# Moving the first loads, the root tables, the last rows and one store of a hybrid decoder step

## The chip, the cores and the metric

The kernel runs on one core of a Trainium2 chip. The core has a matrix engine (TensorE, PE in the rows; its weight loads are PEld), a vector engine (VectorE, DVE), a scalar engine for functions and copies (ScalarE, ACT), a slower general engine (GpSimd, POOL), and a queue engine (SyncE, SP) that issues most transfers. A "q" behind an engine's name is its sequencer: waiting, and issuing transfers. The metric is device microseconds (us) for one execution; lower is better.

## The reference

One decoder layer for 1024 prompt tokens and 8 sampled tokens, width 1024. All of it but two places lies outside the change: the norm at the very start and the norm at the very end.

```python
def _rms_norm(x, g):
    xf = x.astype(jnp.float32)
    y = xf * lax.rsqrt(jnp.mean(xf * xf, axis=-1, keepdims=True) + EPS)
    return (y * g.astype(jnp.float32)).astype(x.dtype)
...
    h = _rms_norm(x, norm_mix)
    proj = jnp.einsum('bld,de->ble', h, w_in).astype(f32)
...
    pe = jnp.einsum('blp,pd->bld', p, w_pl_proj)
    x = x + pe * jax.nn.sigmoid(jnp.einsum('bld,de->ble', _rms_norm(x, norm_pl), w_pl_gate))
...
        return _rms_norm(x, norm_final), [jnp.stack(lst) for lst in new]
```

## The kernel before

Tokens are cut into nine tiles: eight of 128 prompt tokens and one of the 8 sampled ones. Inside, activations lie with the 1024 features on the partitions (eight blocks of 128) and the 1032 tokens along the row, split into a high and a low part, so that each dense product is three matmuls (`mm`, line 69): weight-high by act-high, weight-high by act-low, weight-low by act-high. A weight slice of 1024 x 128 is loaded as `wraw`, cast to `wh` on ScalarE (line 138), and the rest `wl` is formed on VectorE (line 139). `dense` runs over token chunks of 344.

**Opening.** SP asks for the token tiles `xt` (line 210), and between them for the norm gains (`gain_cols`, five small loads into `r0`, line 117) and three narrow column slices of `w_in` (line 216, into `wsm`, 48 columns in use). Then come three groups of three token tiles (`PARTS`). Per tile: the sum of squares on ScalarE (line 224), the root (line 225), the reciprocal and the scaled copy `xn` on VectorE (lines 226, 227). Per group and feature block k: three transposes of `xn` on TensorE into a PSUM tile (line 233), then the high part on ScalarE (line 235) and the low part on VectorE (line 236), both with the gain column of the block. The first products, for `wsm`, and those of the first gate slices run between the groups as soon as their chunk is there.

**Ending.** The last token group (264 tokens) goes through eight gate products. For each, `gate_add` scales on VectorE (line 1276), takes the sigmoid on ScalarE (line 1277), multiplies by `pe` (line 1280) and adds to the residual `x2` (line 1281; its tile is called `acc` in the rows). Then `final(tt)` for the tiles 6, 7 and 8 (tile 8 has the 8 sampled rows): transposes back (line 1294), two halves of a sum of squares (line 1296), the root (line 1298), the reciprocal (line 1299), the scaling with the final gain `gf` (line 1302) and a store (line 1303).

The framework's scheduler sets the order of instructions on each engine from the order of the code and from dependencies; each engine runs its own list strictly in that order, and waits on counters of the other engines. Of two activations that need different function tables (square, copy and root live in one, sigmoid in another) a table load stands ahead of the second.

Of the kernel before, what the change touches and what calls it, by code (L numbers as in the profile page):

```python
# [8 lines left out]
F32 = mybir.dt.float32  # L9
F32R = mybir.dt.float32r  # L10
AF = mybir.ActivationFunctionType
ALU = mybir.AluOpType
# [4 lines left out]
P = 128  # L17
# [6 lines left out]
PARTS = ((0, 384), (384, 384), (768, 264))  # L24
# [15 lines left out]
def hybrid_step(  # L40
# [9 lines left out]
    V, S, G, TE = nc.vector, nc.scalar, nc.gpsimd, nc.tensor  # L50
    dma = nc.sync.dma_start
# [4 lines left out]
    cp = ctx.enter_context(tc.tile_pool(name="cp", bufs=1, reuse_waits="tile"))  # L56
# [12 lines left out]
        TE.matmul(o, l, r, start=start, stop=stop)  # L69


    ident = cp.tile([P, P], F32, name="ident")
    make_identity(nc, ident)
    ones = cp.tile([P, P], F32, name="ones")
# [31 lines left out]
    def gain(base, k):  # L106
        return gcols[:, base + k : base + k + 1]
# [6 lines left out]
    def gain_cols(pool):  # L114
        r0 = pool.tile([41, P], F32, name="r0")
        for src, o, n in ((norm_mix, 0, 8), (norm_ffn, 8, 8), (norm_pl, 16, 8), (ssm_norm, 24, 16), (gdn_norm, 40, 1)):
            dma(r0[o : o + n, :], src[0].rearrange("(k p) -> k p", p=P))
        to_cols(r0, gcols, 41)

    def conv_cols(pool):  # L120
        r1 = pool.tile([120, P], F32, name="r1")
        for j in range(4):
            dma(r1[24 * j : 24 * j + 24, :], ssm_conv_w[0][j].rearrange("(k p) -> k p", p=P))
        dma(r1[96:120, :], ssm_conv_b[0].rearrange("(k p) -> k p", p=P))
        r2 = pool.tile([96, P], F32, name="r2")
        for j in range(4):
            dma(r2[24 * j : 24 * j + 24, :], gdn_conv_w[0][j].rearrange("(k p) -> k p", p=P))
        to_cols(r1, cwm, 120)
        to_cols(r2, cwg, 96)
# [72 lines left out]
    with (  # L202
        tc.tile_pool(name="p0", bufs=1, side="right", reuse_waits="tile") as p0,
        tc.tile_pool(name="p0x", bufs=4, side="right", reuse_waits="tile") as p0x,
    ):
        xts = []
        for tt in range(9):
            n = P if tt < 8 else NB
            xt = p0x.tile([P, D], F32, name="xt", bufs=9)
            dma(xt[:n], x_prompt[0, tt * P : tt * P + P, :] if tt < 8 else x_sample[:, 0, :])  # L210
            xts.append(xt)
            if tt == 0:
                gain_cols(p0)
            if tt == 3:
                for o, c0, m in ((0, COL_DT, 32), (R_B, COL_BETA, 8), (R_A, COL_A, 8)):
                    dma(wsm[:, :, o : o + m], w_in[:, c0 : c0 + m].rearrange("(k p) f -> p k f", p=P))
        for g in range(3):
            t0, tn = PARTS[g]
            xns = []
            for tt in range(3 * g, 3 * g + 3):  # L220
                n, xt = (P if tt < 8 else NB), xts[tt]
                xn = p0x.tile([P, D], F32, name="xn", bufs=6)
                ss = p0x.tile([P, 1], F32, name="ss", bufs=9)
                S.activation(xn[:n], xt[:n], AF.Square, accum_out=ss[:n])
                S.activation(ss[:n], ss[:n], AF.Sqrt, bias=b_eps[:n], scale=1.0 / D)
                V.reciprocal(ss[:n], ss[:n])
                V.tensor_scalar(xn[:n], xt[:n], ss[:n], None, ALU.mult)
                xns.append((xn, n))
            for k in range(KD):
                pool, name = ((pt, "pt"), (py, "py"), (pz, "pz"), (pt, "pt"), (py, "py"))[k % 5]  # L230
                t = pool.tile([P, 512], F32, name=name)
                for j, (xn, n) in enumerate(xns):
                    TE.transpose(t[:, j * P : j * P + n], xn[:n, k * P : k * P + P], ident[:n, :n])
                h, l = (a[:, t0 : t0 + tn] for a in hacts[k])
                S.activation(h, t[:, :tn], AF.Copy, scale=gain(G_MIX, k))
                V.scalar_tensor_tensor(l, t[:, :tn], gain(G_MIX, k), h.bitcast(F32), ALU.mult, ALU.subtract)
        conv_cols(p0)
# [72 lines left out]
    with tc.tile_pool(name="pr", bufs=1, side="right", reuse_waits="tile") as pr:  # L310
# [67 lines left out]
        for hh in range(2):  # L378
            q = slice(64 * hh, 64 * hh + 64)
# [711 lines left out]
    for tt in range(9):  # L1091
        n = P if tt < 8 else NB
# [3 lines left out]
        for k in range(2):  # L1096
            TE.transpose(t[:, k * P : k * P + n], pr_[:n, k * P : k * P + P], ident[:n, :n])
            ts = slice(tt * P, tt * P + n)
# [44 lines left out]
    for f in range(8):  # L1143
# [16 lines left out]
        if 1 <= f < 5:  # L1160
            q = 2 * (f - 1)
# [21 lines left out]
    def roots(sqs, rb, t0, tn):  # L1183

        ts = slice(t0, t0 + tn)
        t = pt.tile([P, 512], F32, name="pt")
        G.tensor_tensor(rb[:, ts], rb[:, ts], sqs[:, ts], ALU.add)
        mm(t[:, :tn], ones, rb[:, ts])
        S.activation(rb[:, ts], t[:, :tn], AF.Sqrt, bias=b_eps, scale=1.0 / D)
        V.reciprocal(rb[:, ts], rb[:, ts])  # L1190
# [73 lines left out]
    gf = nrm.tile([P, D], F32, name="gf")  # L1264
    dma(gf, norm_final.partition_broadcast(P))

    def gate_add(f, t0, tn, o):

        ts = slice(t0, t0 + tn)
        if t0 < PARTS[2][0] and f < 2:  # L1270
            if f == 0:
                roots(sqs2, rb2, t0, tn)
            elif t0 == 0:
                roots(sqs2, rb2, *PARTS[2])
        gt = b2.tile([P, 384], F32, name="pg", tag="sg")
        V.tensor_tensor(gt[:, :tn], rb2[:, ts], o, ALU.mult)  # L1276
        S.activation(gt[:, :tn], gt[:, :tn], AF.Sigmoid)
        pe_ = b2.tile([P, 384], F32, name="pe2", tag="xf")
        dma(pe_[:, :tn], pe_d[f, :, ts])
        V.tensor_tensor(gt[:, :tn], gt[:, :tn], pe_[:, :tn], ALU.mult)  # L1280
        V.tensor_tensor(x2[:, f, ts], x2[:, f, ts], gt[:, :tn], ALU.add)

    def final(tt):
        n = P if tt < 8 else NB
        ts = slice(tt * P, tt * P + n)
        ss = nrm.tile([P, 3], F32, name="fss", bufs=3)
        xo = b2.tile([P, D], F32, name="xo", tag="xf" if tt == 8 else "lt")
        halves = []
        for q in range(2):
            pool, name = (pd, "pd") if tt == 8 else ((pt, "pt"), (py, "py"))[q]  # L1290
            t = pool.tile([P, 512], F32, name=name)
            halves.append(t)
            for k in range(4):
                TE.transpose(t[:n, k * P : k * P + P], x2[:, 4 * q + k, ts], ident)
            sq = b2.tile([P, 512], F32, name="fsq", tag="sg")
            S.activation(sq[:n], t[:n], AF.Square, accum_out=ss[:n, q : q + 1])
        V.tensor_tensor(ss[:n, 2:3], ss[:n, 0:1], ss[:n, 1:2], ALU.add)
        S.activation(ss[:n, 2:3], ss[:n, 2:3], AF.Sqrt, bias=b_eps[:n], scale=1.0 / D)
        V.reciprocal(ss[:n, 2:3], ss[:n, 2:3])
        for q in range(2):  # L1300
            c = slice(512 * q, 512 * q + 512)
            V.scalar_tensor_tensor(xo[:n, c], halves[q][:n], ss[:n, 2:3], gf[:n, c], ALU.mult, ALU.mult)  # L1302
        dma(y_prompt[0, ts, :] if tt < 8 else y_sample[:, 0, :], xo[:n])


    for part in (PARTS[:2], PARTS[2:]):
        for f in range(8):
            if len(gws) == f:
                w = slb.tile([P, 2, 8, P], F32R, name="gw", tag="parts")
                with tc.high_priority(offset=2000):  # L1310
                    raw = wp.tile([P, 8, P], F32, name="wraw")
                    dma(raw, w_pl_gate[:, f * P : f * P + P].rearrange("(k p) f -> p k f", p=P))
                    S.copy(w[:, 0], raw)  # L1313
                    V.tensor_tensor(w[:, 1], raw, w[:, 0].bitcast(F32), ALU.subtract)  # L1314
                gws.append([(w[:, 0, k], w[:, 1, k]) for k in range(8)])
            dense(gws[f], h3acts, lambda t0, tn, o: gate_add(f, t0, tn, o), part)
        for tt in range(6) if len(part) == 2 else range(6, 9):
            final(tt)
# [38 lines left out]
```

## Time and profile before

| | |
|---|---|
| median of three runs | 2700.68 us (2695.79 to 2703.67) |
| the profiled execution: its time / its span | 2698.8 us / 2697.1 us |
| TensorE busy | 2628.7 us, 97% of the span |
| VectorE, ScalarE, GpSimd busy | 57%, 38%, 10% |
| first transpose of a token tile | 10.74 us |
| first dense product | 18.01 us |
| last dense product ends | about 2683.3 us |

Times within the trace count from the span's start. Between the first dense product and the last TensorE has hardly a gap, so the change is read in two places: the 18 us ahead of the first product with the 20 us behind it, and the 14 us behind the last product.

### The profile page before, as it was taken

How to read it: one execution, taken by the hardware profiler on the slowest of the kernel's cores; microseconds unless marked ns; L12 is line 12 of the kernel's file. 1: busy time of each engine (PE TensorE's matmuls, PEld its weight loads, DVE VectorE, ACT ScalarE, POOL GpSimd, SP SyncE). 2: the span in 40 equal slices, each digit the busy share in tenths (PEclk: the TensorE clock that was granted, in tenths of full speed). 3: DMA queues.
4: the chain of work that ended last, by engine and by line, in shares of the span. 5: the costliest groups of instructions: out<-in, count | busy, mean ns of one | idle time of the engine just before them, and what ended most of it. 6: DMA issues, size and time to landing. Idle time of an engine off the chain costs nothing.

```text
span 2697.1 us, 43777 instructions
## 1 busy us (share of the span) xinstructions
PE 2628.7 (97%) x17431; PEld 2544.5 (94%) x17431; DVE 1546.1 (57%) x2757; ACT 1024.8 (38%) x2080; POOL 256.9 (10%) x495
## 2 busy tenths in 40 slices
PE   7999999999989999999999999999999999999998
PEld 7999999989989899898999999999999999999998
DVE  6677897588657576565445575434343333333465
ACT  5555556364364373343332235322112121212243
POOL 0111222121110110210000000010000000000020
PEclk9999999999999999999999999999999999999999
DMA  3345445455453453477664457411111111111122
GB/s 123 119 151 173 140 154 157 105 116 153 112 127 114 104 149 101 103 209 200 189 187 139 117 183 246 128 45 46 42 53 44 51 44 51 44 52 43 45 89 94
DMA packets 456666, 306.34 MB, mean 114 GB/s; under 512 B 44049, under 2 KB 430010, under 8 KB 455438
## 3 DMA queue, kind: packets, MB, share of 16 engines
q1 hardware_dynamic: 454062, 295.13, 38.5%
q10 hardware_dynamic: 2400, 8.42, 0.8%
q8 instruction: 137, 2.24, 0.3%
q14 instruction: 67, 0.55, 0.1%
HBM read 227.17 MB, written 76.31 MB: 113 GB/s over the span
## 4 chain that ended last, share of the span: by engine, by line
PE 49%; DVE 1%; DMA 1%; ACT 1%; issue 1%; SPq 0%; DVEq 0%; ACTq 0%
PE pd L69 45%; PE py L69 2%; PE pt L69 1%; DMA wraw<-in_w_pl_gate_dram 0%; PE pt L1139 0%; DMA kg<-ktok_d 0%; PE pz L69 0%; DVE gw L1314 0%; PE pt L968 0%; DMA pr<-in_p_prompt_dram 0%; DMA wraw<-in_w_pl_proj_dram 0%; DVE y L187 0%; DMA mg<-y_d 0%; DVE xo L1302 0%; ACT gw L1313 0%
## 5 line engine op out<-in xcount | busy, mean ns | idle before, releaser
L69 PE MATMUL pd<-h,wh 128*128 128x344 f32 x6384 | 1542.4, 323 | 18.3 <-ACT wh L138 11.1
L69 PEld LDWEIGHTS pd<-h,wh 128*128 128x128 f32 x6384 | 1106.4, 189 | 31.7 <-ACT wh L138 13.4
L69 PE MATMUL pd<-h,wl 128*128 128x344 f32 x3192 | 1030.7, 323 | 1.8 <-DVE wl L139 0.7
L69 PEld LDWEIGHTS pd<-h,wl 128*128 128x128 f32 x3192 | 602.8, 189 | 7.0 <-DVE wl L139 5.3
L138 ACT CAST wh<-wraw 128x512 fp32r<-128x512 f32 (+1 forms) x386 | 234.4, 609 | 847.5 <-PE pd L69 812.4
L139 DVE TENSOR_TENSOR wl<-wraw,wh 128x512 fp32r<-128x512 f32 (+1 forms) x386 | 265.1, 688 | 342.2 <-ACT wh L138 338.5
L69 PE MATMUL pd<-gu,wh 128*128 128x344 f32 (+2 forms) x1056 | 249.2, 320 | 0.1
L69 PE MATMUL pd<-y,wh 128*128 128x344 f32 x768 | 187.7, 325 | 0.0
L69 PEld LDWEIGHTS pd<-gu,wh 128*128 128x128 f32 x1056 | 182.3, 188 | 0.5 <-DVE acc L1195 0.4
L69 PE MATMUL pd<-gu,wl 128*128 128x344 f32 (+2 forms) x528 | 168.9, 320 | 0.0
L709 ACT ACTIVATE ab<-ab,ncolA 128x128 f32<-128x128 f32 x256 | 81.8, 391 | 142.1 <-POOL ab L705 136.0
L69 PEld LDWEIGHTS pd<-y,wh 128*128 128x128 f32 x768 | 133.4, 190 | 1.2 <-issue 0.2
L69 PE MATMUL pd<-y,wl 128*128 128x344 f32 x384 | 125.2, 326 | 0.0
L1246 DVE TENSOR_TENSOR acc<-acc,pd 128x344 f32<-128x344 f32 x120 | 61.2, 512 | 103.9 <-PE pd L69 103.5
L422 ACT COPY raw<-pd 128x344 f32<-128x344 f32 x144 | 62.5, 438 | 149.6 <-PE pd L69 137.2
L1181 POOL TENSOR_TENSOR sqs<-sqs,sqt 128x1032 f32<-128x1032 f32 x12 | 30.5, 2542 | 923.9 <-ACT sqt L1180 923.9
L1225 DVE TENSOR_TENSOR lt<-rb,pd 128x344 f32<-128x344 f32 x66 | 33.8, 513 | 141.2 <-PE pd L69 141.2
L69 PEld LDWEIGHTS pd<-gu,wl 128*128 128x128 f32 x528 | 99.2, 188 | 0.0
L436 DVE SCALAR_TENSOR_TENSOR ca<-raw,cwm,ca 128x1056 f32<-128x1056 f32 x72 | 95.9, 1332 | 2.0
L436 DVE SCALAR_TENSOR_TENSOR ca<-raw,cwg,ca 128x1056 f32<-128x1056 f32 x72 | 96.5, 1341 | 0.8
L69 PE MATMUL pd<-h,gw 128*128 128x384 f32 (+1 forms) x576 | 94.3, 322 | 1.5 <-DVE pg L1276 1.5
L69 PEld LDWEIGHTS pd<-h,gw 128*128 128x128 f32 x576 | 91.2, 188 | 2.5 <-DVE pg L1276 1.9
(391 smaller groups left out, 3458.1 us busy)
## 6 DMA issues: line engine op xcount, KB each, us to landing
wraw<-in_w_in_dram SPq DMA_DIRECT2D x88, 512.0 KB
wraw<-in_w_ffn_in_dram SPq DMA_DIRECT2D x44, 512.0 KB
ab<-acum_d SPq DMA_DIRECT2D x32, 512.0 KB
out_dram<-sd SPq DMA_DIRECT2D x48, 256.0 KB
wraw<-in_w_ffn_out_dram SPq DMA_DIRECT2D x40, 256.0 KB
sg_d<-mg SPq DMA_DIRECT2D x16, 516.0 KB
bb<-rk_d SPq DMA_DIRECT2D x8, 1024.0 KB
sd<-in_state_ssm_dram SPq DMA_DIRECT2D x32, 256.0 KB
```

What stands on the lines that cost most here:

```text
L69: TE.matmul(o, l, r, start=start, stop=stop)
L138: S.copy(wh[:, :n], raw[:, k0 : k0 + n])
L139: V.tensor_tensor(wl[:, :n], raw[:, k0 : k0 + n], wh[:, :n].bitcast(F32), ALU.subtract)
L422: S.copy(raw[:, 3 + t0 : 3 + t0 + n], o[:, :n])
L436: V.scalar_tensor_tensor(ca, raw[:, j : j + CONVN], w[j], ca, ALU.mult, ALU.add)
L709: S.activation(ab[:, h], ab[:, h], AF.Exp, bias=ncolA[:, c, h0 + h : h0 + h + 1])
L1181: G.tensor_tensor(sqs[:, ts], sqs[:, ts], sq[:, :tn], ALU.add)
L1225: V.tensor_tensor(dst[:, t0 : t0 + tn], rb[:, t0 : t0 + tn], o, ALU.mult)
L1246: V.tensor_tensor(a, a, o, ALU.add)
```

## The change

Four edits. (1) The first three token tiles are asked for ahead of the gain vectors, and the narrow slices of `w_in` move one tile further back. (2) A tiny tile `warm` is set, and a square root of it stands first on ScalarE, so that the table with the root is the one loaded first. (3) Behind the last sigmoid of the kernel another tiny root, of the first column of `gt`, brings the same table back. (4) In `final`, the rows of tile 8 are scaled by the reciprocal on ScalarE and multiplied by the final gain on GpSimd, and the store of tile 7 is issued from ScalarE's queue.

```diff
+    warm = cp.tile([P, 2], F32, name="warm")
+    V.memset(warm, 1.0)
+    S.activation(warm[:, 0:1], warm[:, 0:1], AF.Sqrt)
     ident = cp.tile([P, P], F32, name="ident")
...
-            if tt == 0:
+            if tt == 2:
                 gain_cols(p0)
-            if tt == 3:
+            if tt == 4:
                 for o, c0, m in ((0, COL_DT, 32), (R_B, COL_BETA, 8), (R_A, COL_A, 8)):
                     dma(wsm[:, :, o : o + m], w_in[:, c0 : c0 + m].rearrange("(k p) f -> p k f", p=P))
...
         S.activation(gt[:, :tn], gt[:, :tn], AF.Sigmoid)
+        if f == 7 and t0 == PARTS[2][0]:
+            S.activation(warm[:, 1:2], gt[:, 0:1], AF.Sqrt)
...
-            V.scalar_tensor_tensor(xo[:n, c], halves[q][:n], ss[:n, 2:3], gf[:n, c], ALU.mult, ALU.mult)
-        dma(y_prompt[0, ts, :] if tt < 8 else y_sample[:, 0, :], xo[:n])
+            if tt == 8:
+                S.activation(xo[:n, c], halves[q][:n], AF.Copy, scale=ss[:n, 2:3])
+                G.tensor_tensor(xo[:n, c], xo[:n, c], gf[:n, c], ALU.mult)
+            else:
+                V.scalar_tensor_tensor(xo[:n, c], halves[q][:n], ss[:n, 2:3], gf[:n, c], ALU.mult, ALU.mult)
+        (S.dma_start if tt == 7 else dma)(y_prompt[0, ts, :] if tt < 8 else y_sample[:, 0, :], xo[:n])
```

Line numbers behind the first edit are higher by three in the changed kernel, and by more behind the others. The head of SP's list, with the counters that each transfer waits for (transfers report to eight completion counters in turn, DMAHW0 to DMAHW7, so that the ninth waits for the first), before:

```order
L210 DMA xt<-in_x_prompt_dram 128x1024
L117 DMA r_113<-in_norm_mix_dram 8x128
L117 DMA r_113<-in_norm_ffn_dram 8x128
...
L146 DMA wraw<-in_w_in_dram 128x8x128 [waits DMAHW1_49]
L216 DMA wraw<-in_w_in_dram 128x8x32 [waits DMAHW2_49,Pool_49]
```

and in the changed kernel:

```order
L213 DMA xt<-in_x_prompt_dram 128x1024 x3
L120 DMA r_120<-in_norm_mix_dram 8x128
...
L213 DMA xt<-in_x_prompt_dram 128x1024 [waits DMAHW0_49]
L149 DMA wraw<-in_w_in_dram 128x8x128 [waits DMAHW1_49]
L213 DMA xt<-in_x_prompt_dram 128x1024 [waits DMAHW2_49]
L219 DMA wraw<-in_w_in_dram 128x8x32 [waits DMAHW3_49,Pool_49]
```

Three tiles now stand at the head; the fifth tile waits for the third to have landed, and the narrow slices stand behind it.

The head of ScalarE's list, without waits (`xn,ss` is the sum of squares of a token tile, `ss` alone the root, `h` the high part), before:

```order
L224 ACT_TABLE_LOAD
L224 ACTIVATE xn,ss<-xt 128x1024 x2
L225 ACT_TABLE_LOAD
L225 ACTIVATE ss<-ss,b_eps 128x1 x2
L224 ACTIVATE xn,ss<-xt 128x1024
L225 ACTIVATE ss<-ss,b_eps 128x1
L224 ACTIVATE xn,ss<-xt 128x1024
L235 ACTIVATE h_101<-pt,gcols 128x384
...
L225 ACTIVATE ss<-ss,b_eps 128x1
L138 CAST wh<-wraw 128x512
L224 ACTIVATE xn,ss<-xt 128x1024
```

and in the changed kernel:

```order
L74 ACT_TABLE_LOAD
L74 ACTIVATE warm<-warm 128x1
L227 ACTIVATE xn,ss<-xt 128x1024 x3
L228 ACTIVATE ss<-ss,b_eps 128x1 x3
L227 ACTIVATE xn,ss<-xt 128x1024
L238 ACTIVATE h_104<-pt,gcols 128x384
...
L228 ACTIVATE ss<-ss,b_eps 128x1
L227 ACTIVATE xn,ss<-xt 128x1024
L141 CAST wh<-wraw 128x512
```

One table load is gone; the first three roots stand behind the third square; and the square of the fifth tile has moved ahead of the first cast of a weight.

The end of the lists of ScalarE and then of VectorE and GpSimd in the changed kernel, with waits (`Activation` counts ScalarE's finished instructions; before, ScalarE's list has the table load behind the two squares, VectorE's ends with two scalings of `xo<-pd` 8x512, and GpSimd's has nothing here):

```order
L1280 ACTIVATE pg<-pg 128x264 [waits DVE_49]
L1282 ACT_TABLE_LOAD
L1282 ACTIVATE warm<-pg 128x1 [waits Activation_49]
L1301 ACTIVATE fsq,fss<-py 128x512 [waits PE_49]
...
L1303 ACTIVATE fss<-fss,b_eps 8x1 [waits DVE_49]
L1312 DMA out_dram<-xo 128x1024 [waits DMAHW4_49,DVE_49]
L1308 ACTIVATE xo<-pd,fss 8x512 [waits DMAHW5_49,DMAHW3_49,DMAHW7_49,DMAHW1_49,DVE_49]
L1308 ACTIVATE xo<-pd,fss 8x512
```

```order
L1285 TENSOR_TENSOR pg<-pg,pe_26022 128x264 [waits DMAHW2_49,Activation_49]
L1286 TENSOR_TENSOR acc<-acc,pg 128x264 [waits DVE_49]
...
L1304 RECIPROCAL fss<-fss 8x1 [waits Activation_49]
```

The tiny root reads `pg`, which the multiply on VectorE then overwrites, so that the multiply's count on ScalarE is one higher than before: it waits for the tiny root too. The two copies of tile 8 stand behind the store of tile 7 on ScalarE, and the last work ahead of the last store is now GpSimd's.

## Rows read from the trace of the kernel before

**Rows 1.** The page, its first part: busy time, share, instructions.

```profile
PE 2628.7 (97%) x17431; PEld 2544.5 (94%) x17431; DVE 1546.1 (57%) x2757; ACT 1024.8 (38%) x2080; POOL 256.9 (10%) x495
```

**Rows 2.** Windows: length, PE, PEld, DVE, ACT, POOL busy, PEclk, DMA share, GB/s.

```profile
2.00:4.00 2.00, 0.00 (x0) 0.00 (x0) 0.98 (x3) 0.09 (x1) 0.64 (x3) 1.00 0.74 263
4.00:11.00 7.00, 0.56 (x2) 0.44 (x3) 1.40 (x5) 5.14 (x10) 0.00 (x0) 1.00 0.97 312
6.00:7.00 1.00, 0.00 (x0) 0.00 (x0) 0.00 (x0) 0.06 (x1) 0.00 (x0) 1.00 1.04 406
18.00:24.20 6.20, 6.13 (x21) 5.61 (x22) 5.29 (x12) 5.70 (x13) 0.13 (x2) 0.51 0.49 141
24.20:40.00 15.80, 15.56 (x102) 13.40 (x100) 10.83 (x27) 9.42 (x22) 0.15 (x2) 1.00 0.04 9
```

**Rows 3.** Timeline of SP's queue, opening: start, length, what, count.

```profile
0.82 0.39 SPq L210 DMA_DIRECT2D xt<-in_x_prompt_dram  x1
3.00 1.70 SPq L210 DMA_DIRECT2D xt<-in_x_prompt_dram  x3
5.29 6.37 SPq L216 DMA_DIRECT2D wraw<-in_w_in_dram  x3
```

**Rows 4.** Timeline of ScalarE, opening; in brackets idle time before and releaser.

```profile
4.38 1.06 ACT L224 ACTIVATE xn<-xt 128x1024 f32<-128x1024 f32 x1 [2.28 <-DMA xt<-in_x_prompt_dram]
...
6.94 1.06 ACT L224 ACTIVATE xn<-xt 128x1024 f32<-128x1024 f32 x1 [1.42 <-DMA xt<-in_x_prompt_dram]
...
8.11 1.28 ACT L225 ACT_TABLE_LOAD   x1
...
13.39 0.58 ACT L235 ACTIVATE h<-pt,gcols 128x384 fp32r<-128x384 f32 x1 [1.10 <-PE pt L233]
...
17.29 0.67 ACT L138 CAST wh<-wraw 128x512 fp32r<-128x512 f32 x1
...
25.70 0.58 ACT L235 ACTIVATE h<-pt,gcols 128x384 fp32r<-128x384 f32 x1 [2.00 <-PE pt L233]
```

**Rows 5.** Timeline of VectorE, the last two token tiles of the opening.

```profile
31.18 1.40 DVE L227 TENSOR_SCALAR xn<-xt,ss 128x1024 f32<-128x1024 f32 x2
```

**Rows 6.** Timeline of TensorE, opening.

```profile
10.74 0.47 PE L233 MATMUL pt<-ident,xn 128*128 128x128 f32 x1 [5.01 <-DVE xn L227]
...
12.93 0.42 PE L233 MATMUL pt<-ident,xn 128*128 128x128 f32 x1
...
18.01 0.94 PE L69 MATMUL pd<-h,wh 128*128 128x344 f32 x2 [1.74 <-ACT wh L138]
```

**Rows 7.** Timeline of ScalarE, ending.

```profile
2684.37 0.41 ACT L1277 ACTIVATE pg<-pg 128x264 f32<-128x264 f32 x1
...
2687.48 1.28 ACT L1298 ACT_TABLE_LOAD   x1
2688.77 0.29 ACT L1298 ACTIVATE fss<-fss,b_eps 128x1 f32<-128x1 f32 x1
```

**Rows 8.** Timeline of VectorE, ending.

```profile
2684.81 0.43 DVE L1280 TENSOR_TENSOR pg<-pg,pe 128x264 f32<-128x264 f32 x1 [1.04 <-ACT pg L1277]
...
2692.06 0.74 DVE L1302 SCALAR_TENSOR_TENSOR xo<-py,fss,gf 128x512 f32<-128x512 f32 x1
...
2692.89 1.40 DVE L1302 SCALAR_TENSOR_TENSOR xo<-pd,fss,gf 8x512 f32<-8x512 f32 x2
```

**Rows 9.** Timeline of SP's queue, ending: the last three stores, first start, whole length.

```profile
2690.79 3.82 SPq L1303 DMA_DIRECT2D out_dram<-xo  x3
```

**Rows 10.** Groups by shape, GpSimd: count, busy us, mean ns, idle before and releaser.

```profile
L1187 POOL TENSOR_TENSOR rb<-rb,sqs 128x384 f32<-128x384 f32 x2 | 3.2, 1604 | 0.1
L1187 POOL TENSOR_TENSOR rb<-rb,sqs 128x344 f32<-128x344 f32 x3 | 2.9, 980 | 5.6 <-ACT rb L1177 5.5
...
L1187 POOL TENSOR_TENSOR rb<-rb,sqs 128x264 f32<-128x264 f32 x1 | 0.8, 761 | 2.9 <-ACT rb L1177 2.9
```

## The prediction

> **What bounds the kernel now.** The page's busy shares come first: TensorE is busy 2628.7 us of a span of 2697.1 us [rows 1]. So a change that leaves the middle as it is can only move the two ends, and I read these engine by engine on the timeline.
>
> In the opening the reader is to see a chain. The first token tile is squared at 4.38 us, the second, which was asked for only at 3.00 us behind the gains, at 6.94 us [rows 3, 4]. Behind it a table load of 1.28 us holds the first root until 9.39 us [rows 4]. The first scaled tile reaches TensorE at 10.74 us, and the first PSUM tile is complete after twelve transposes, the last of them at 12.93 us [rows 6]; ScalarE takes it over at 13.39 us, makes eight high parts, and casts the first weight at 17.29 us [rows 4]. TensorE's first product starts at 18.01 us, released by that cast [rows 6]. From there on TensorE is busy 6.13 of 6.20 us, at a granted clock of 0.51 (the lower level, 1.2 GHz), and then 15.56 of 15.80 us at 1.00 (2.4 GHz) [rows 2].
>
> In the ending the chain behind the last product runs sigmoid (2684.37), multiply on VectorE (2684.81), add, one transpose, squares, table load (2687.48 to 2688.76), root (2688.77), and two scalings for each tile, of which the last, of tile 8, are done at 2694.29 us [rows 7, 8]. The last store is issued there: the row of the three stores ends at 2694.61 [rows 9].
>
> **The change part by part: the opening.** *Landing of the third tile.* All three first roots now stand behind the square of the third tile, so the third landing sets the start, where before it was the second landing and the load. Three tiles are 1.57 MB. Transfers move from about 2.0 us on, at 263 GB/s while one tile is under way, at 312 as a mean later, at 406 in the best single microsecond [rows 2]. The first tile with the gains (0.55 MB) needs 2.1 us at 263, so 4.1, and the square starts at 4.38 [rows 4]: 0.3 us more. The third therefore lands at 2.0 + 5.0 + 0.3 = 7.3 us at the mean, which I take since three tiles under way resemble that stretch; at 263 it is 8.3, at 406 it is 6.2.
>
> *First group.* Before, from the second landing to TensorE's first transpose took 3.80 us, with the table load of 1.28 in it [rows 4, 6]. Without the load it is 2.5: TensorE starts at 9.8 instead of 10.74. The scaled third tile is ready by 11.55 (two more scalings of 0.7 and the copy of the gains behind the first one at 9.75, with the halves of 1.40 from [rows 5]). In the new order the first PSUM tile is complete after eight transposes and the gains' own instead of twelve, so it is not held by TensorE's pace, and ScalarE starts its high parts at about 12.05, 1.34 us earlier than 13.39. But the square of the fifth tile now stands ahead of the first cast, about 1.05 us with its read-out. From 13.39 to the cast took 3.90 us [rows 4], so the cast comes at 12.05 + 3.90 + 1.05 = 17.0, and the first product 0.72 us behind it, as before, at 17.7: 0.3 us earlier. The gains, which stand second on TensorE's list, land behind the third tile, by about 7.5, over 2 us ahead of need.
>
> *Second and third group.* In TensorE's new list 16 products instead of 20 stand ahead of the sixth tile's transposes; at the higher clock 102 matmuls take 15.56 us [rows 2], 0.15 each, so four are 0.6 us. The second group's high parts then start 0.9 us ahead of 25.70 [rows 4]. The fifth tile waits for the third landing, and the narrow slices' three issues, 6.37 us [rows 3], move from 5.29 to about 7.7 and end at 14.1. The sixth tile is asked for only then and lands, with the 3.56 us of the first tile (0.82 to 4.38), at 17.7, when ScalarE comes to it at 17.8; TensorE wants it at 24.5, so nearly 3 us more are in hand there. For the third group three scalings instead of two are left on VectorE behind the second, 0.7 us more, part of which falls into its present wait for the last square: I work out 32.1 for the last scaled tile instead of 32.58 [rows 5]. I book **0.5 us gained** for the opening. Its ends come from the landing: 0.5 lost at 8.3, 1.6 gained at 6.2, all passed on to the end, since TensorE's later gaps are few [rows 1]. Memset and tiny root at the start lie in the idle 2.28 us ahead of 4.38 [rows 4].
>
> **The ending.** *The table load behind the last sigmoid.* It looks free, since ScalarE idles there before. But the tiny root reads the tile that VectorE's multiply overwrites, and by the wait lists the multiply waits for it. Sigmoid ends at 2684.78, load 1.28, root 0.29 [rows 7]: the multiply starts at 2686.40 instead of 2684.81 [rows 8], 1.59 us late, and with it the add, the transpose and both squares. At the root 1.29 us of load are gone from the path (2687.48 to 2688.77 [rows 7]). Net **0.30 us lost** instead of 1.3 won.
>
> *Tile 8 and the stores.* Before, tile 7's scaling ends at 2692.80 and tile 8's 1.49 us later [rows 8]. Now, counted from the end of tile 7: ScalarE wakes (0.03) and issues tile 7's store (0.39, as the first issue on SP [rows 3]); the first copy, 0.68 (between 0.58 for 384 columns [rows 4] and 0.77 in proportion for 512); hand-over 0.04; two multiplies on GpSimd, since the second copy hides behind the first of them; wake of SP 0.03. No GpSimd multiply of 8 x 512 is in the trace. From 264 to 344 columns its rows go from 761 to 980 ns, 2.74 ns a column, so 1.44 us for 512 [rows 10]. Below, VectorE's 0.73 for the same shape (two in 1.40) [rows 8]; above, the rate of the 384 row, 1604 ns, so 2.14 [rows 10]. I take 1.44, since nothing else then runs beside it, as in the 264 and 344 rows. Sum 0.03 + 0.39 + 0.68 + 0.04 + 2.88 + 0.03 = 4.05, against 1.49: **2.56 us lost** (1.15 to 3.95). VectorE is free from the end of tile 7 on, so nothing covers the two multiplies. The store of tile 7 starts about where it did, and SP was free for it, so its own queue buys nothing.
>
> The Trainium skill (GPSIMD Engine Reference, section "Engine selection") says that elementwise work belongs on VectorE, and that GpSimd takes about twice as long with two inputs; its section on elementwise cost gives 4497 ns for 2048 columns. An estimate from this page of the Trainium skill is 1.12 us for 512 columns, by which the sum below would be 0.6 us smaller. The trace's rows give 1.44; no row here shows the very shape.
>
> **Sum.** 0.30 + 2.56 - 0.5 = +2.4 us. The profiled execution of 2698.8 us (span 2697.1 and 1.7 around it) would become 2701.2. It lies 1.9 us under the median of the three runs, 2700.68, so the forecast of a median is **2703.1 us**. The three runs span 7.9 us, 0.3%: a measurement of this kernel can hardly tell less than 0.3%, 8.1 us, from no change.
>
> **Rivals.**
> *A. The load hides.* If the multiply did not wait for the tiny root, the squares would start about 0.2 late and 1.28 would leave the path: 1.37 better, +1.0, 2701.7 us. For it: 1.4 us of idle on ScalarE. Against it: the wait list. Chance 0.05.
> *B. The opening passes on more.* Tiles land at the best rate and the higher clock is granted earlier: 1.6 us by the landing, and each microsecond less at 0.51 gives half a microsecond back [rows 2], so up to 3 us, and GpSimd at its lower end. Net -2, 2698.7 us. For it: 1.3 us at the first high parts. Against it: the fifth square ahead of the cast. Chance 0.17.
> *C. The other side: the clock.* If the transposes and first products come with holes, the higher level could be granted much later than 24.2 us. Each later microsecond of the 15.8 busy ones costs half [rows 2], so with 2.9 us of ending the time is over 0.3% slower from a rise at about 35 us on (10.6 / 2 + 2.9 = 8.2): 2709 us or more. For it: the sixth tile arrives with only 0.1 us to spare on ScalarE. Against it: TensorE needs it 3 us later. Chance 0.05.
> *D. The middle size:* landing at 8.3, GpSimd at 2.14 and a sixth tile that holds ScalarE for up to 3 us: +5 to +8, 2707 us. Chance 0.07.
> *E. Faster by over 0.3%.* The opening could give that only if a later wait of TensorE vanished with it; its idle time in all is 68 us [rows 1]. Chance 0.04.
>
> **How the numbers follow.** My forecast, net between -0.2 (1.45 - 1.6) and +4.8 (4.25 + 0.5), has 0.62. Cases A, B and D stay within 0.3%, so no change has 0.91, slower by over 0.3% 0.05 (C), faster 0.04 (E). The range takes the bounds of the net about 2700.7 with 4 to 5 us for the spread of runs: 2695.5 to 2709.5 us.
>
> **What would show it.** After: the third square starts at about 7.3 us with one load ahead of it; the high parts start near 12 and the first product near 17.7; the clock rises near 24. In the ending the multiply starts about 3.1 us behind the last product's end, released by the tiny root; tile 8's two multiplies on GpSimd take about 1.4 us each, and the last store is issued some 14 us behind the last product instead of 11. The forecast is wrong if the first product moves by more than 1 us either way, if GpSimd takes well under a microsecond, or if the middle changes its length.

## The result, and the profile after

The changed kernel takes 2703.24 us (median of 22 runs, 2696.79 to 2710.61) against 2699.36 us before (22 runs, 2692.67 to 2703.67): ratio 1.0017, 95% interval 1.0010 to 1.0025, no change by the 0.3% of the prediction. The forecast was 2703.1 us. The profiled execution is the slowest of the 22, 2710.61 us with a span of 2708.9 us, so its whole length says little; its two ends are read engine by engine.

The changed kernel's busy times (against [rows 1]), then its windows: length, PE, PEld, DVE, ACT, POOL busy, clock, DMA share, GB/s (against [rows 2]).

```profile
PE 2630.3 (97%) x17431; PEld 2548.2 (94%) x17431; DVE 1547.3 (57%) x2756; ACT 1026.0 (38%) x2083; POOL 258.9 (10%) x497
```

```profile
4.00:11.00 7.00, 0.63 (x2) 0.36 (x3) 1.70 (x5) 5.04 (x11) 0.00 (x0) 1.00 1.03 337
18.00:24.20 6.20, 5.54 (x26) 5.26 (x27) 4.20 (x8) 5.16 (x13) 0.13 (x2) 0.72 0.37 105
24.20:40.00 15.80, 14.48 (x98) 12.97 (x95) 11.84 (x29) 10.46 (x25) 0.15 (x2) 1.00 0.07 17
```

TensorE's busy time has grown by 1.6 us; the clock of the stretch from 18 us is 0.72 instead of 0.51. The opening on ScalarE (against [rows 4]), with idle time and releaser in brackets:

```profile
0.81 1.28 ACT L74 ACT_TABLE_LOAD   x1 [0.81 <-PEq L1353]
...
7.90 1.06 ACT L227 ACTIVATE xn<-xt 128x1024 f32<-128x1024 f32 x1 [1.00 <-DMA xt<-in_x_prompt_dram]
...
8.96 0.65 ACT L228 ACTIVATE ss<-ss,b_eps 128x1 f32<-128x1 f32 x3
...
12.79 0.58 ACT L238 ACTIVATE h<-pt,gcols 128x384 fp32r<-128x384 f32 x1 [2.15 <-PE pt L236]
...
16.97 1.04 ACT L227 ACTIVATE xn<-xt 128x1024 f32<-128x1024 f32 x1
...
18.01 0.60 ACT L141 CAST wh<-wraw 128x512 fp32r<-128x512 f32 x1
...
24.53 0.58 ACT L238 ACTIVATE h<-pt,gcols 128x384 fp32r<-128x384 f32 x1 [1.37 <-PE pt L236]
```

and on TensorE (against [rows 6]):

```profile
18.66 0.58 PE L69 MATMUL pd<-h,wh 128*128 128x344 f32 x2 [2.40 <-ACT wh L141]
...
40.09 0.59 PE L69 MATMUL pd<-h,wh 128*128 128x344 f32 x2 [0.99 <-ACT x L330]
```

The load no longer stands between the squares and the roots, yet the first product starts 0.65 us later than before: the third landing (7.90) and the fifth tile's square (16.97) hold the cast. The second group's high parts start 1.17 us earlier (24.53 against 25.70). I call the last row, the product behind the copy of the biases, **the mark**: the first product that waits for something else than the norm, in every kernel here. In the kernel before it is this row:

```profile
40.95 0.59 PE L69 MATMUL pd<-h,wh 128*128 128x344 f32 x2 [0.99 <-ACT x L327]
```

So in these two profiles the opening is 0.86 us shorter.

The ending on ScalarE, VectorE, GpSimd and the two queues (against [rows 7, 8, 9]):

```profile
2694.21 1.28 ACT L1282 ACT_TABLE_LOAD   x1
2695.50 0.20 ACT L1282 ACTIVATE warm<-pg 128x1 f32<-128x1 f32 x1
...
2698.22 0.29 ACT L1303 ACTIVATE fss<-fss,b_eps 128x1 f32<-128x1 f32 x1
...
2702.28 0.37 ACTq L1312 DMA_DIRECT2D out_dram<-xo  x1
2702.85 1.25 ACT L1308 ACTIVATE xo<-pd,fss 8x512 f32<-8x512 f32 x2 [2.06 <-DMA out_dram<-xo]
```

```profile
2692.75 0.43 DVE L1279 TENSOR_TENSOR pg<-rb,pd 128x264 f32<-128x264 f32 x1 [1.10 <-PE pd L69]
2695.74 0.43 DVE L1285 TENSOR_TENSOR pg<-pg,pe 128x264 f32<-128x264 f32 x1 [2.55 <-ACT warm L1282]
...
2701.50 0.74 DVE L1311 SCALAR_TENSOR_TENSOR xo<-py,fss,gf 128x512 f32<-128x512 f32 x1
```

```profile
2703.61 2.47 POOL L1309 TENSOR_TENSOR xo<-xo,gf 8x512 f32<-8x512 f32 x2 [103.78 <-ACT xo L1308]
```

```profile
2700.23 6.17 SPq L1312 DMA_DIRECT2D out_dram<-xo  x2
```

The last gate scaling of the kernel before:

```profile
2683.34 0.43 DVE L1276 TENSOR_TENSOR pg<-rb,pd 128x264 f32<-128x264 f32 x1 [1.10 <-PE pd L69]
```

I count the ending from the last gate scaling on VectorE (2692.75, the first row of its fence; 2683.34 before) to the end of the row of SP's stores: 13.65 us, against 11.27 before, so +2.38. Inside it the multiply starts 2.99 us behind the gate scaling (1.47 before), released by the tiny root; the root 5.47 (5.43 before); and GpSimd's two multiplies take 2.47. Both ends together cost 2.38 - 0.86 = 1.5 us in these profiles.

### The profile page after: what moved, and what is told of

Read it like the earlier page. It is cut to its first block, busy times and chain, and to the rows that moved or that the text cites. A ratio compares the mean times of both kernels' runs of the same rounds, so it can differ in the third digit from the quotient of the medians.

```text
span 2708.9 us, 43787 instructions
## 1 busy us (share of the span) xinstructions
PE 2630.3 (97%) x17431; PEld 2548.2 (94%) x17431; DVE 1547.3 (57%) x2756; ACT 1026.0 (38%) x2083; POOL 258.9 (10%) x497
## 4 chain that ended last, share of the span: by engine, by line
PE 66%; DMA 7%; ACT 3%; DVE 2%; issue 1%; POOL 1%; SPq 0%; POOLq 0%; ACTq 0%; DVEq 0%
PE pd L69 59%; PE py L69 3%; DMA ab<-acum_d 2%; PE pt L69 2%; PE pz L69 1%; DMA out_dram<-so 1%; ACT ab L712 1%; DMA DB<-dd_d 1%; DMA wraw<-in_w_pl_gate_dram 1%; DMA mg<-y_d 0%; ACT sdt L616 0%; ACT wh L141 0%; POOL ab L708 0%; DMA kg<-ktok_d 0%; DVE wl L142 0%
```

## The experiments

Each kernel was timed 11 or 12 times, in three sessions beside runs of before that the kernels of a session share. A ratio of these comparisons has an interval of about 0.1% either side, 2.3 to 3.5 us, wider than most effects here; what an edit did is read from the ends of its trace, and the timings serve for the middle.

### Does a moved layout matter?

`pad_only` is before with an unused tile of 8 bytes, which moves most later tiles by 32 bytes as the change's tile does:

```diff
+    pad = cp.tile([P, 2], F32, name="pad")
+    V.memset(pad, 1.0)
```

> The kernel before with one unused tile of 8 bytes a partition, set once, ahead of all others, which moves nearly all SBUF tiles by 32 bytes, as the tiny tile of the change does. Theory 1 (only the two ends count, the rest of the difference is scatter of the runs): no difference, 0 +- 2 us, and both ends of the trace as before (last product to last store 11.0 us). Rival S (the moved tiles make the middle slower): +2 to +4 us with both ends as before.

Measured: 2703.61 us, ratio 1.001 (1.0001 to 1.0018). Its windows and its mark, with the same lists of the opening as before:

```profile
18.00:24.20 6.20, 5.79 (x28) 5.42 (x29) 5.12 (x12) 5.94 (x14) 0.13 (x2) 0.72 0.61 188
```

```profile
40.16 0.58 PE L69 MATMUL pd<-h,wh 128*128 128x344 f32 x2 [0.99 <-ACT x L329]
```

The reader is to see that the clock of 0.72 comes without any change of the opening, and that the mark stands at 40.16 instead of 40.95 with it. The time alone, 2.5 us over before with an ending of 11.27 as before, is what the rival asks for; the next kernel tests it from the other side.

Two profiles of one and the same kernel, `load_hidden` and `hidden_again` below, differ in the same way. The windows from 16 to 26 us of before, `early_root`, `load_hidden` and `hidden_again`:

```profile
16.00:26.00 10.00, 8.21 (x39) 7.42 (x38) 7.41 (x16) 8.00 (x19) 0.13 (x2) 0.66 0.51 170
16.00:26.00 10.00, 9.26 (x44) 8.44 (x45) 7.16 (x16) 8.06 (x19) 0.13 (x2) 0.67 0.48 159
16.00:26.00 10.00, 7.71 (x44) 7.50 (x45) 7.46 (x15) 8.85 (x21) 0.13 (x2) 0.83 0.50 161
16.00:26.00 10.00, 8.11 (x38) 7.94 (x38) 6.23 (x14) 7.61 (x18) 0.13 (x2) 0.66 0.47 151
```

Three of the thirteen profiles (before, `early_root`, `hidden_again`) have 0.66 or 0.67 there, the other ten 0.83. So before's own profile had a long stretch at the lower level, and the rise against [rows 2] is not the change's doing.

The four profiles with the old opening have the mark at 40.95, 40.16, 40.27 and 40.23, mean 40.40; the seven with the new one at 38.75 to 40.34, mean 39.67. The opening is worth **0.73 us** by these means. They mix the two clocks; like with like it is 0.67 at 0.83 (40.22 to 39.55, three and six profiles) and 0.61 at 0.66 (40.95 to 40.34, one each).

`no_shift` is the changed kernel with `warm` in the slack of another small tile, all addresses as before:

```diff
...
-    b_epsq = bias_col(128.0 * EPS, "b_epsq")
+    beq = cp.tile([P, 4], F32, name="b_epsq")
+    b_epsq, warm = beq[:, 0:1], beq[:, 1:3]
...
```

> The changed kernel with its tiny tile put into unused bytes beside another constant, so that no other tile moves. Theory 1: the same ends as the changed kernel (opening 0.85 us earlier at 40 us, ending 2.4 us longer), so +1.5 us against before, and not to be told from the changed kernel beyond 2 us. Rival S: +1.5 us as well, but the changed kernel's own +3.9 is then explained by the moved tiles, so the two differ by 2 to 4 us, in the middle.

Measured: 2705.95 us, ratio 1.0015 (1.0006 to 1.0024), as the changed kernel; mark 39.88, ending 13.66. The cost is there without moved tiles, so they are not what the change costs.

### The opening, taken apart

`opening_only` has the opening of `no_shift` (loads and first root) and the ending of before.

> Before with the opening alone (the order of the loads and the first root, tiny tile in unused bytes; ending as before). Theory 1: first product later (18.7 instead of 18.0 us) but the products of the opening done 0.8 to 0.9 us earlier at 40 us, ending 11.0 us from the last product to the last store, -0.9 us in all. Rival O (the later first product costs as much as it moved, 0.65 us): +0.6 us at 40 us.

Measured: 2702.75 us, ratio 1.0007 (0.9996 to 1.0018); mark 38.75, ending 11.55. No gain shows in the time, and the ending is 0.28 longer than before, though no line of it was changed. Its second square starts later:

```profile
2689.70 0.60 ACT L1300 ACTIVATE fsq<-py 128x512 f32<-128x512 f32 x1 [1.69 <-PE pd L1298]
```

It is released by the last transpose of tile 8 (`pd`), where in before the transposes of its own tile release it (1.42 us of idle time, `<-PE py`). `loads_only` has the same releaser and an ending of 11.56. So the new order of the loads also changes a wait at the other end of these two kernels; in the changed kernel and `no_shift` it does not (`<-PE py` there).

`loads_only` changes only the order of the loads (`tt == 2` and `tt == 4`, no early root):

> The kernel before with only the order of the first loads changed; no early root, so a table load of 1.28 us stands between the third square and the first root. Theory 1: the gain of 0.9 us at the 40 us mark comes from the early table; then everything up to the first product is 1.28 us later than in the changed kernel (first transpose 11.65, first product 19.9), and the 40 us mark lies 0.4 us behind that of before. Theory 2: it comes from the new order of the lists (fewer products ahead of the sixth tile, a shorter stretch at 0.5 of the clock); then the 40 us mark lies 0.3 us or more ahead of before although the first product starts 1.9 us later. Ending as before, last store 10.96 behind the last gate scaling.

Measured: 2704.3 us, ratio 0.9994 (0.9982 to 1.0005). ScalarE, then TensorE:

```profile
8.11 1.06 ACT L224 ACTIVATE xn<-xt 128x1024 f32<-128x1024 f32 x1 [1.40 <-DMA xt<-in_x_prompt_dram]
...
9.27 1.28 ACT L225 ACT_TABLE_LOAD   x1
```

```profile
19.91 0.59 PE L69 MATMUL pd<-h,wh 128*128 128x344 f32 x2 [2.40 <-ACT wh L138]
...
41.34 0.59 PE L69 MATMUL pd<-h,wh 128*128 128x344 f32 x2 [0.99 <-ACT x L327]
```

`early_root` is the other half, the loads in their old order:

```diff
...
+    V.memset(warm, 1.0)
+    S.activation(warm[:, 0:1], warm[:, 0:1], AF.Sqrt)
...
```

> The kernel before with only the first tiny root (its tile in slack, addresses unchanged); the loads are asked for in the old order, all lists stay but for the table load that is gone. Theory: the early table is the whole gain of the opening, and the new order of the loads costs some of it: the first transpose at 9.4 (10.74 before), the first product at 16.7 to 16.9 (18.0 to 18.2 in the four kernels with the opening of before), the mark near 40 us (first product behind the copy of the biases) 1.0 to 1.3 ahead of the 40.16 to 40.95 of those four, so at 39.0 to 39.4; in the changed kernel it is 40.09. Rival: the third tile's landing caps it, and the mark gains less than 0.5: then the order of the loads is needed for the gain. Ending as before, last store 10.96 behind the last gate scaling.

Measured: 2701.91 us, ratio 1.0005 (0.9995 to 1.0015). ScalarE, then TensorE:

```profile
7.99 0.46 ACT L229 ACTIVATE ss<-ss,b_eps 128x1 f32<-128x1 f32 x2
...
11.96 0.58 ACT L239 ACTIVATE h<-pt,gcols 128x384 fp32r<-128x384 f32 x1 [0.90 <-PE pt L237]
```

```profile
16.58 0.94 PE L69 MATMUL pd<-h,wh 128*128 128x344 f32 x2 [1.74 <-ACT wh L142]
...
39.46 0.42 PE L69 MATMUL pd<-h,wh 128*128 128x344 f32 x1 [0.99 <-ACT x L331]
```

The early table alone brings the first product from 18.0 to 18.2 (four profiles of before's opening) to 16.58. The mark comes to 39.46, 0.94 ahead of the mean of the four, and 1.49 ahead of before's own profile, the one with the same clock from 16 to 26 us. The new loads alone put the first product at 19.91 and the mark at 41.34, 0.94 behind the mean and 1.12 behind the three with the same clock (40.22). So **the table is the gain, and the loads cost**: the third landing keeps the first product at 17.72 to 18.66 in the seven profiles that have both, 1.1 to 2.1 later than with the table alone. Part of it is won back behind the first product, where the new order of the lists needs 21.0 to 21.4 us to the mark in the six of the seven at 0.83, against 22.0 to 22.2 in the three of before's opening at 0.83. Like with like, the old loads with the early table have the mark 0.88 ahead of both edits together (39.46 against 40.34 in `hidden_again`); that is one profile each, and no kernel tried has them with the hidden load of the next section.

### The ending, taken apart

`tail_root` is before with only the tiny root behind the last sigmoid:

```diff
+        if f == 7 and t0 == PARTS[2][0]:
+            S.activation(warm[:, 1:2], gt[:, 0:1], AF.Sqrt)
```

> The kernel before with one edit: the tiny root behind the last sigmoid, its tile in slack, addresses unchanged. Theory: the multiply starts 3.0 us behind the last gate scaling (1.47 before) and the root stands 5.47 behind (5.43 before): the load has left one place and stands in another, ending +0.04 us, last store 11.0 us behind. Rival, the term of the prediction: +0.30, root 5.73 behind. Time: within 0.1% of before.

Measured: 2703.81 us, ratio 0.9988 (0.9977 to 1.0000). VectorE, then ScalarE:

```profile
2688.55 0.43 DVE L1278 TENSOR_TENSOR pg<-rb,pd 128x264 f32<-128x264 f32 x1 [1.10 <-PE pd L69]
2691.54 0.43 DVE L1284 TENSOR_TENSOR pg<-pg,pe 128x264 f32<-128x264 f32 x1 [2.55 <-ACT b_epsq L1281]
```

```profile
2694.01 0.29 ACT L1302 ACTIVATE fss<-fss,b_eps 128x1 f32<-128x1 f32 x1
```

The multiply starts 2.99 us behind the gate scaling and the root 5.46: the load has left the root's path and stands on the multiply's, and the ending is 11.30 instead of 11.27. That the wait is the cause is shown by the next kernel.

`load_hidden` keeps opening and tiny root, leaves tile 8 and the stores as before, and writes the last product to `pe_`'s tile, so that the multiply overwrites nothing that the tiny root reads:

```diff
-        V.tensor_tensor(gt[:, :tn], gt[:, :tn], pe_[:, :tn], ALU.mult)
-        V.tensor_tensor(x2[:, f, ts], x2[:, f, ts], gt[:, :tn], ALU.add)
+        last = f == 7 and t0 == PARTS[2][0]
+        pr_ = pe_ if last else gt
+        V.tensor_tensor(pr_[:, :tn], gt[:, :tn], pe_[:, :tn], ALU.mult)
+        V.tensor_tensor(x2[:, f, ts], x2[:, f, ts], pr_[:, :tn], ALU.add)
```

> Opening alone, and the tiny root behind the last sigmoid, but the last multiply writes into the tile of pe and no longer over the tile that the tiny root reads; tile 8 and the stores as before. Theory 1 (the tiny root holds the multiply by the tile it reads): the multiply starts 1.5 us behind the last product as before, the root 1.3 us earlier than before, last product to last store 9.8 us instead of 11.0, -2.1 us in all. Rival: if the multiply still starts 3.0 us behind the last product, it was the table load itself that held it, and the ending stays at 11.0 us.

Measured: 2700.42 us, ratio 0.999 (0.9981 to 0.9999). VectorE, then ScalarE:

```profile
2687.23 0.43 DVE L1280 TENSOR_TENSOR pg<-rb,pd 128x264 f32<-128x264 f32 x1 [1.10 <-PE pd L69]
2688.70 0.43 DVE L1288 TENSOR_TENSOR pe<-pg,pe 128x264 f32<-128x264 f32 x1 [1.04 <-ACT pg L1281]
```

```profile
2688.69 1.28 ACT L1283 ACT_TABLE_LOAD   x1
...
2691.23 0.29 ACT L1306 ACTIVATE fss<-fss,b_eps 128x1 f32<-128x1 f32 x1
```

Load and multiply now start together, the root stands 4.00 us behind the gate scaling instead of 5.43, and the ending is 9.84: **1.43 us** less.

`tile8_alone` is before with the ScalarE copies and GpSimd multiplies of tile 8, all stores on SP.

> The kernel before with one edit: tile 8 is scaled on ScalarE and multiplied on GpSimd; its store and that of tile 7 stay on SP, nothing else moves. Theory: the copies and the two multiplies (1.24 us each) stand behind tile 8's reciprocal, which stands behind tile 7's scalings: about 0.2 + 0.62 + 0.1 + 2.47 + 0.03 = 3.4 us behind the end of tile 7's scaling, against 1.49 before, so the last store about 12.9 us behind the last gate scaling (10.96 before, 13.36 in the changed kernel): +1.9, and the 0.45 left are the store's issue in ScalarE's list ahead of the copies. Rival: that issue cost nothing, and the last store stands 13.3 us behind here too. In the middle all lists are those of before: if the 2 to 3 us that the ends do not explain come from the new opening, the median is 1.9 above before; if they are scatter, it may be anything from 0 to +5.

Measured: 2704.6 us, ratio 1.0003 (0.999 to 1.0015). VectorE's last row, ScalarE, GpSimd:

```profile
2690.40 0.74 DVE L1306 SCALAR_TENSOR_TENSOR xo<-py,fss,gf 128x512 f32<-128x512 f32 x1
2691.05 0.14 DVE L1299 RECIPROCAL fss<-fss 8x1 f32<-8x1 f32 x1
```

```profile
2691.23 1.25 ACT L1303 ACTIVATE xo<-pd,fss 8x512 f32<-8x512 f32 x2 [1.55 <-DVE fss L1299]
```

```profile
2691.98 2.47 POOL L1304 TENSOR_TENSOR xo<-xo,gf 8x512 f32<-8x512 f32 x2 [102.95 <-ACT xo L1303]
```

The copies start 0.09 us behind the end of tile 7 (2691.14), where in the changed kernel they start 0.61 behind it (2702.24 to 2702.85), past the store on ScalarE's queue. The ending is 13.09, so copies and multiplies cost 1.82 and the store ahead of them 0.53 (13.65 less 13.09, less 0.03 of the tiny root). The bracket of the changed kernel's copies names the landing of tile 6's store, but by the trace's own records the last update of its counter came at 2702.87, 0.02 us behind the start of the copy (0.01 behind it in `no_shift` and `after_again`), so it was not what released the copy. From the end of the issue (2702.65) to the copy (2702.85) ScalarE's sequencer runs two instructions that wait for counters of transfers, 0.20 us in all three profiles: the store costs its issue of 0.37 and these waits, which stand behind it in the list.

`half8` is `load_hidden` with only the first half of tile 8 by that way, its reciprocal put between tile 7's scalings, and the second half on VectorE:

> The version with the hidden load (opening and tail root as in the changed kernel, the last product written to another tile, stores on SP), and in tile 8 only the first half goes by a copy on ScalarE and a multiply on GpSimd, with its reciprocal between tile 7's two scalings; the second half stays on VectorE. Theory: both halves run side by side, copy 0.60, multiply 1.24, so the last store stands about 9.4 us behind the last gate scaling (9.52 with the load hidden alone, 10.96 before, 13.36 in the changed kernel). Rival: GpSimd's multiply is slower beside VectorE's scaling, 1.5 us or more, and the last store stands at 9.7 or later. Time: about 1.5 us below before by the ends.

Measured: 2701.5 us, ratio 0.999 (0.9977 to 1.0002). VectorE, then GpSimd:

```profile
2695.80 0.73 DVE L1316 SCALAR_TENSOR_TENSOR xo<-pd,fss,gf 8x512 f32<-8x512 f32 x1
```

```profile
2696.01 1.25 POOL L1314 TENSOR_TENSOR xo<-xo,gf 8x512 f32<-8x512 f32 x1 [99.34 <-ACT xo L1313]
```

The multiply takes 1.25 us beside VectorE's scaling, as in `tile8_alone` (two in 2.47, a little overlapped), so the rival falls; but the ending, 9.78, is only 0.06 shorter than with the load hidden alone.

### The middle

> The changed kernel once more, beside before. Both ends together cost 2.4 - 0.8 = 1.6 us, 0.06%. If the 2 to 4 us more in the first comparison belong to the kernel, the ratio is 1.0015 or more again; if they are scatter of the comparison, which moved other kernels with the same middle between -3 and +3 us, it may be anything from 0.9995 to 1.002. The ends in the trace: mark near 40 us at 39.9 to 40.1, last store 13.3 to 13.4 behind the last gate scaling.

Measured for `after_again`: 2708.27 us against 2701.03, ratio 1.0019 (1.0009 to 1.0029), mark 39.27, ending 13.65.

> The version with the hidden load once more (opening and tail root of the change, the last product written to another tile, tile 8 and stores as before). By its ends it is 0.8 + 1.44 = 2.2 us under before and 3.8 us under the changed kernel of the same call: ratio to before 0.999, with an interval of about 0.001 either side; mark near 40 us at 39.5 to 39.9, last store 9.5 behind the last gate scaling.

Measured for `hidden_again`: 2699.08 us, ratio 0.9998 (0.9985 to 1.0011), mark 40.34, ending 9.83. What each ratio leaves over, once the ends are taken off (mean mark of its kind of opening less 40.40, plus ending less 11.27; 0.1% is 2.7 us):

| session | kernel: left over, us |
|---|---|
| the result above | changed kernel +2.9 (4.6 - 1.65) |
| first | `pad_only` +2.7, `no_shift` +2.4, `opening_only` +2.3, `load_hidden` -0.5 |
| second | `tile8_alone` -1.0, `tail_root` -3.3, `loads_only` -2.8, `half8` -0.5 |
| third | `early_root` +2.3, `after_again` +3.5, `hidden_again` +1.6 |

`pad_only`, `tile8_alone` and `tail_root` have the lists of before in the whole middle, and yet they lie 6 us apart; the sign mostly goes with the session, whose kernels share the runs of before. So most of what is left over is scatter of the comparison. The changed kernel is the one that shows it three times with the same sign (with `no_shift`), +2.4 to +3.5 us, at a resolution of about 2.4. The profiles lean the same way without settling it: from the mark to the last gate scaling the five with the old loads take 2641.4 to 2648.3 us (mean 2644.2), the eight with the new ones 2641.0 to 2652.7 (mean 2647.7). The same middle stretch in before and in the changed kernel, as windows and then by what TensorE's two largest waits were for (us, times, longest):

```profile
500.00:1700.00 1200.00, 1165.90 (x8092) 1107.20 (x8091) 747.39 (x1565) 508.51 (x1192) 138.11 (x314) 0.99 0.54 149
```

```profile
500.00:1700.00 1200.00, 1159.09 (x8043) 1101.48 (x8043) 747.58 (x1558) 505.95 (x1188) 137.51 (x314) 0.99 0.53 148
```

```profile
PE pd L69 <- ACT wh L138: 9.4, 6, 3.2
PE pd L69 <- ACT zt L456: 6.1, 3, 2.2
```

```profile
PE pd L69 <- ACT zt L459: 12.6, 3, 4.9
PE pd L69 <- ACT wh L141: 7.2, 7, 1.9
```

TensorE is busy 6.8 us less there in the changed kernel's profile, at the same clock of 0.99, in waits that the other has too, only of other lengths; in `hidden_again`, with the same opening, it is busy 1166.87 us, more than before. Whether the new start of the lists lengthens these waits by a few microseconds on the mean stays open.

## Why the prediction was right

The verdict was right, and so was the mechanism of the ending; the sum of the two ends was +2.4 us as booked and +1.65 as measured (2.38 - 0.73). That the median came within 0.2 us of the forecast is luck: the median of before was 1.3 us lower than the one the forecast started from, and by the medians the kernel became 3.9 us slower, of which the ends explain 1.65.

- **The landing of the third tile** was booked at 7.3 us (6.2 to 8.3) and was 7.90 here; in the seven profiles of the new opening the third square starts at 7.16 to 7.90, mean 7.59. The step that failed is the one that carried this on to "the first product at 17.7, 0.3 us earlier": it was 18.66, 0.65 later, and on the mean of the seven 18.23 against 18.10 of the four. Of the 0.96 from 17.7 to 18.66, 0.6 is the landing, and 0.27 are waits for transposes between the eight high parts (12.79 to 16.78 is 3.99, against 3.72 before).
- **The gain of the opening** was booked at 0.5 and was 0.73 on the mean, 0.6 to 0.7 like with like, but not at the first product: the term that held is the shorter list ahead of the sixth tile. The second group was booked 0.9 us earlier; the 1.17 of these two profiles holds the clock as well, and like with like it is 1.0 (24.97 to 23.97 on the mean at 0.83, 25.70 to 24.75 at 0.66). That edits 1 and 2 work against each other was only in it as the fifth square's delay of the cast: alone, the loads lengthen the opening by 1.1.
- **The tiny root holds the multiply** as the wait list said: 2.99 us behind the gate scaling, forecast about 3.1. The term was mis-sized: booked +0.30, measured +0.04 at the root. The tiny root takes 0.20, not the 0.29 of the row that I took; and a load between squares and root cost 0.15 more than its own 1.28: before, it starts at 2687.48, when the read-out of the last square has ended, while the root without a load starts 0.11 ahead of that end in the changed kernel (2698.22 against 2698.33). `load_hidden` won 1.43 by moving it. Rival A (the load hides) is false for the change and true once the overwritten tile is another.
- **Tile 8** was booked at 2.56 and cost 2.35, of which 1.82 are the copies and multiplies and 0.53 the store ahead of the copies (booked 0.42, without the waits behind its issue). GpSimd's multiply took 1.25 us against 1.44 by the slope of [rows 10]. The estimate from the Trainium skill (GPSIMD Engine Reference, section "Engine selection" and the cost beside it), 1.12, was nearer; what the section says of the choice holds here: the same shape takes 0.73 us on VectorE, so GpSimd needs 1.7 times as long.
- The Trainium skill (ScalarE: Activation LUTs, section "What ACT_TABLE_LOAD costs") puts a switch at 1283 ns and a drain of about 1380 ns more. The trace agrees with the load, 1.28, and not with the drain, and the trace decides here: the load of 2694.21 starts 0.02 behind the sigmoid's end (2694.19), it ends at 2695.49, and the next activation starts at 2695.50.
- **Rival B** saw the clock as part of the gain. The higher clock of 18 to 24 us did come, but `pad_only` shows it without the change. Its sum was off too: 0.30 + 1.15 - 3 is -1.55, not -2. **Rival C** did not occur: the lowest clock of the stretch behind 24.2 us in any profile was 0.98, in `loads_only`.
- **The middle** was taken as unchanged. The spread of one kernel's runs, 6 to 16 us from lowest to highest, is larger than the whole effect; the prediction's margin of 4 to 5 us for it was needed.

## What to carry to other kernels

A table load moved into idle time is worth its 1.4 us only if nothing waits for the dummy activation that pulls it: give that activation an input that nobody overwrites next. Try an earlier table and an earlier transfer apart: here the table alone gained about 1.5 us and the transfers' order alone lost 1.1, each read from profiles with the same clock. Where a stretch can run at either level of the clock, compare only profiles that had the same one. An engine that is idle at the end is no help if it is the slower one: two 8-row multiplies on GpSimd cost more than VectorE's scalings, and a store issued on the queue of the engine that has the next work delayed that work by 0.5 us here. Of the versions tried, the hidden load with tile 8 left on VectorE is 2.2 us under before by its ends; its timings, 0.999 and 0.9998, can hardly show that.

## What the hardware showed that was not expected

- The same opening lists gave the mark at 40.16 to 40.95 us (old) and 38.75 to 40.34 (new). The scatter is of executions and not only of programs: `load_hidden` and `hidden_again` are one kernel and have it at 39.50 and 40.34, the changed kernel and `after_again` at 40.09 and 39.27. The landing of the third tile and the length of the stretch at the lower clock both vary.
- GpSimd's 8 x 512 multiply takes 1.25 us, alone or beside VectorE's scaling, while rows of 128 partitions with 344 columns take 0.98 [rows 10].
